# Batched matrix product on one core: an uneven store moves from batch 11 to batches 1 and 2

## The chip, the cores and the metric

The kernel runs on one core of a Trainium2 chip. The metric is the device time of one execution in microseconds; the time before is 124.91 us, the median of three runs (124.76 to 125.31). A profile of one execution and its trace stand beside the times. Engines are named as the profile names them: PE (TensorE), DVE (VectorE), ACT (ScalarE), POOL (GpSimd), SP (SyncE). The 16 DMA engines that move data between HBM and SBUF are another thing; they are numbered 0 to 15 here.

## The reference

Sixteen independent products of 512 x 512 float32 matrices, the second one transposed:

```python
def setup_inputs():
    batch, m, k, n = 16, 512, 512, 512
    return {
        "a": np.random.randn(batch, m, k).astype(np.float32),
        "b": np.random.randn(batch, n, k).astype(np.float32),
    }

def reference(a: np.ndarray, b: np.ndarray) -> np.ndarray:
    return np.matmul(a, b.transpose(0, 2, 1)).astype(np.float32)
```

33.6 MB are read and 16.8 MB are written.

## The kernel before

The sixteen batches go in eight pairs (the variable `u`). A load brings both matrices of a pair from one input, 2 MB in rows of 16 KB per partition: load `2u` is the pair's part of `a`, load `2u + 1` its part of `b` (line 86). Seven load slots of `ld` hold them (`NL`), each with its own semaphore. DVE casts a load to bf16 in three pieces (lines 154 to 158), PE transposes 128 x 128 blocks into `tp` (line 223), ACT copies the transposed `a` into `ta` (line 181), DVE the transposed `b` into `tb` (line 168). Then PE multiplies, 32 matmuls for a pair (line 242), and ACT evicts each bank of `ps` into the output buffer `ob` (line 201). `ob` has seven slots (`NO`); batch `n` uses slot `n % 7`, so that the eviction of batch `n` waits until the store of batch `n - 7` has landed (line 198).

The order of work is written out by hand. Each engine has its own list of instructions:

- ACT issues load 0 and loads 2 to 6 at the start, and later loads `2u + 7` and `2u + 8` after its copies of pair `u`'s transposes (lines 192 to 194), ahead of the evictions of that pair. SP issues load 1.
- POOL waits for each load and passes this on to DVE by the semaphore `s_go` (line 108), one load after the other.
- SP waits until load 7 has landed (line 120) and then stores the batches in order, each when ACT has counted it in `s_out` (line 122). A store is one transfer of 1 MB: partition `p` holds output rows `4p` to `4p + 3`, 8 KB that lie together in HBM. The last row of batch 15 is stored apart, at the end (line 263).

Batch 11 (`X`) is stored in parts. Rows 1 and 2 of all partitions are one SP transfer. Rows 0 and 3 of each partition (2 KB each) are divided by partitions: 32 to 95 in one SP transfer; 0 to 15 in four SP transfers of four partitions each, 16 to 19 in a fifth; 20 to 31 and 96 to 127 in eight transfers that POOL issues, in groups of three and eight partitions (lines 112 to 118). Ahead of each pair of these POOL reads five partitions of 128 bytes into `turn`, which nothing uses; this moves on the DMA engine at which POOL's next transfer begins. SP's parts count in `s_x`, POOL's in `s_y`; ACT waits for both at the end of the program (lines 257 and 258), together with the stores of the last seven batches.

`landed(n)` gives the semaphore and the count that show batch `n` stored. `store` makes a transfer from `ob`.

Of the kernel before, what the change touches and what calls it, by code (L numbers as in the profile page):

```python
# [10 lines left out]
def kernel(  # L11
# [6 lines left out]
    nc = tc.nc  # L18
    P = 128
    batch, M, K = a.shape  # L20
    _, N, _ = b.shape
    J = M // P
# [3 lines left out]
    pairs = batch // 2  # L26
    f32 = mybir.dt.float32
    bf16 = mybir.dt.bfloat16
    NL = 7
    NO = 7  # L30
    X = 11

    def sbuf(name, shape, dtype):
        return ctx.enter_context(nc.sbuf_tensor(name, shape, dtype))

    def sem(name):
        return tc.alloc_semaphore(name)

    with tc.tile_critical(no_gpsimd_drain=True):  # L41
# [8 lines left out]
        ob = sbuf("ob", [P, NO, J, N], f32)  # L50
        turn = sbuf("turn", [P, 4, 2, 16], f32)
# [4 lines left out]
        s_ld = [sem(f"s_ld{i}") for i in range(NL)]  # L56
        s_st = [sem(f"s_st{i}") for i in range(NO)]

        s_go = sem("s_go")
# [11 lines left out]
        s_out = sem("s_out")  # L71
        s_x = sem("s_x")
        s_y = sem("s_y")
# [5 lines left out]
            out=ident[:], in_=ident[:], compare_op=mybir.AluOpType.not_equal, fill=1.0,  # L79
# [6 lines left out]
        def load(n, engine):  # L86
            u, slot = n // 2, n % NL
            src = (a if n % 2 == 0 else b)[2 * u:2 * u + 2].rearrange(
                "e (p j) k -> (e p) j k", j=2 * J
            )  # L90
            engine.dma_start(ld[:, slot], src).then_inc(s_ld[slot], 16)

        def landed(n):
            return s_st[n % NO], 16 * (n // NO + 1)

        def store(n, lo=0, hi=J, step=1, part=slice(0, P), engine=nc.sync):
            rows = slice(lo, hi, step)
            return engine.dma_start(  # L98
                out[n].rearrange("(p j) n -> p j n", j=J)[part, rows], ob[part, n % NO, rows]
            )  # L100

        load(0, nc.scalar)
# [1 line left out]
        for n in range(2, NL):  # L104
            load(n, nc.scalar)

        for n in range(2 * pairs):
            nc.gpsimd.wait_ge(s_ld[n % NL], 16 * (n // NL + 1)).then_inc(s_go, 1)  # L108

        nc.gpsimd.wait_ge(s_out, X + 1)
        for i in range(4):
            nc.gpsimd.dma_start(  # L114
                turn[:5, i], a[0, :5, :64].rearrange("p (x k) -> p x k", x=2)[:, :, :16]
            ).then_inc(s_y, 16)
            for part in (slice(20 + i, 32, 4), slice(96 + i, P, 4)):
                store(X, step=J - 1, part=part, engine=nc.gpsimd).then_inc(s_y, 16)

        nc.sync.wait_ge(s_ld[0], 32)  # L120
        for n in range(batch):
            nc.sync.wait_ge(s_out, n + 1)
            if n != X:
                store(n, hi=J if n < batch - 1 else J - 1).then_inc(landed(n)[0], 16)
                continue


            store(n, lo=1, hi=J - 1).then_inc(landed(n)[0], 16)
            store(n, step=J - 1, part=slice(32, 96)).then_inc(s_x, 16)
            for i in range(4):  # L130
                store(n, step=J - 1, part=slice(i, 16, 4)).then_inc(s_x, 16)
            store(n, step=J - 1, part=slice(16, 20)).then_inc(s_x, 16)

        def taker(engine):
            return lambda s, n: engine.wait_ge(s, n).then_inc(s, -n)  # L135
# [9 lines left out]
        with nc.Fori(0, pairs, engines=[dve]) as u:  # L145
            for x, (h, w, s_c, s_w) in enumerate(
# [4 lines left out]
                if x == 0:  # L151
# [4 lines left out]
                    out=h[:, J:, :], in_=src[:, J:, :HK]  # L156
                ).then_inc(s_c, 1)
                nc.vector.tensor_copy(out=w[:], in_=src[:, :, HK:]).then_inc(s_w, 1)  # L158
            for ko in range(KO):
# [5 lines left out]
                if ko == 1:  # L165
# [3 lines left out]
                    out=tb[:, ko, :],  # L169
# [7 lines left out]
        for u in range(pairs):  # L177
            for ko in range(KO):
                nc.scalar.wait_ge(s_ta, KO * u + ko + 1)
                for e in range(2):  # L180
                    c = nc.scalar.copy(  # L181
                        out=ta[:, ko, e * J * P:(e + 1) * J * P].rearrange(
                            "k (j p h) -> k j p h", j=J, h=2
                        ),
                        in_=tp[:, ko % 2, :, e * HP:(e + 1) * HP].rearrange(
                            "k (h j) p -> k j p h", h=2
                        ),
                    )
                c.then_inc(s_ea, 1)


            for n in (2 * u + NL, 2 * u + NL + 1):
                if n < 2 * pairs:
                    load(n, nc.scalar)
            for e in range(2):
                n = 2 * u + e
                if n >= NO:
                    nc.scalar.wait_ge(*landed(n - NO))
                for j in range(J):
                    nc.scalar.wait_ge(s_mm, J * n + j + 1)  # L200
                    c = nc.scalar.copy(  # L201
                        out=ob[:, n % NO, j, :].rearrange("m (p j) -> m p j", j=2 * J),
                        in_=ps[:, j, :].rearrange("m (j p) -> m p j", j=2 * J),
                    )
                    if e == 0:
                        c.then_inc(s_pv, 1)
                    elif j in (0, J - 1):
                        c.then_inc(s_out, 1)
# [4 lines left out]
        with nc.Fori(0, pairs, engines=[pe]):  # L213
            with nc.Fori(0, 2, engines=[pe]):

                for x, (h, s_c, s_t, s_e) in enumerate(
# [3 lines left out]
                    for g in range(2):  # L220
                        take(s_e, 1)
                        for j in range(2 * J):
                            t = nc.tensor.transpose(  # L223
                                tp[:, 2 * x + g, j, :], h[:, j, g * P:(g + 1) * P], ident[:]
                            )
# [6 lines left out]
            for e in range(2):  # L232
                for jj in range(0, J, 2):
                    if e == 1:
                        take(s_pv, 2)
                    for kk in range(0, KO, 2):
                        for j in (jj, jj + 1):
                            for ko in (kk, kk + 1):
                                if (e, jj, j) == (0, 0, 0) and ko >= 2:
                                    nc.tensor.wait_ge(s_ea, ko - 1)  # L240
                                    nc.tensor.wait_ge(s_eb, ko - 1)
                                t = nc.tensor.matmul(  # L242
                                    ps[:, j, :],
                                    ta[:, ko, (e * J + j) * P:(e * J + j + 1) * P],
                                    tb[:, ko, :].rearrange("k (j p) -> k j p", j=2 * J)[
                                        :, :, e * HP:(e + 1) * HP
                                    ],
                                    start=(ko == 0),
                                    stop=(ko == KO - 1),
                                )  # L250
# [3 lines left out]


    with tc.tile_critical(sync_engine=act, no_gpsimd_drain=True):
        nc.scalar.wait_ge(s_x, 16 * 6)
        nc.scalar.wait_ge(s_y, 16 * 12)
        for n in range(batch - NO, batch):
            nc.scalar.wait_ge(*landed(n))  # L260
    waits = nc.cur_bb.bb.instructions[-1]
# [38 lines left out]
```

## Time and profile before

| | us |
|---|---|
| time, median of 3 runs | 124.91 |
| the profiled execution's own time | 125.12 |
| its span, first to last instruction | 123.3 |
| PE busy | 90.2 (73%) |
| DVE busy | 67.9 (55%) |
| ACT busy | 67.9 (55%) |
| POOL busy | 8.5 (7%) |
| load to landing, median | 29.1 (`a`), 26.8 (`b`) |
| 1 MB store to landing, median | 29.0 |
| last load issued, last load landed | 66.68, 99.78 |
| store of batch 14, of 15, of its last row issued | 111.38, 113.54, 114.33 |
| last landing | 122.19 |

The span is cut into 40 slices of 3.08 us; a digit is a busy share in tenths, and the DMA row is the mean of the 16 DMA engines. The profile counts three DMA queues: loads on ACT's queue (q10: 31.46 MB), stores and load 1 on SP's (q1: 18.70 MB), POOL's transfers on a software queue (q0: 0.18 MB). In the waits, "waited for: us in total, times, longest us" stand behind the arrow. A bracket at the end of a timeline line is the time that the engine stood idle before, and what released it; DVEq is DVE's own sequencer, which waits for semaphores. Besides these views the trace keeps a record of each DMA packet.

### The profile page before, as it was taken

How to read it: one execution, taken by the hardware profiler on the slowest of the kernel's cores; microseconds unless marked ns; L12 is line 12 of the kernel's file. 1: busy time of each engine (PE TensorE's matmuls, PEld its weight loads, DVE VectorE, ACT ScalarE, POOL GpSimd, SP SyncE). 2: the span in 40 equal slices, each digit the busy share in tenths (PEclk: the TensorE clock that was granted, in tenths of full speed). 3: DMA queues.
4: the chain of work that ended last, by engine and by line, in shares of the span. 5: the costliest groups of instructions: out<-in, count | busy, mean ns of one | idle time of the engine just before them, and what ended most of it. 6: DMA issues, size and time to landing. Idle time of an engine off the chain costs nothing. (4 is left out here: it accounts for less than half of the span.)

```text
span 123.3 us, 2255 instructions
## 1 busy us (share of the span) xinstructions
PE 90.2 (73%) x768; PEld 54.8 (44%) x768; DVE 67.9 (55%) x96; ACT 67.9 (55%) x130; POOL 8.5 (7%) x18
## 2 busy tenths in 40 slices
PE   0000089999999899989998999999799917996000
PEld 0000078447744764574477347645654506542000
DVE  0000598982896589388918974872977059400000
ACT  0400064567855966696589468765866069656000
POOL 2000000000000000000000000000000039910000
PEclk9999999999999999999999999999999999999965
DMA  4999999999999999999999999999999999999991
GB/s 112 404 425 425 441 431 431 431 431 441 425 436 425 425 361 415 444 423 425 431 433 425 431 423 425 436 444 428 423 423 441 412 423 423 432 397 432 425 407 72
DMA packets 5341, 50.35 MB, mean 408 GB/s; under 512 B 904, under 2 KB 904, under 8 KB 1500
## 3 DMA queue, kind: packets, MB, share of 16 engines
q10 hardware_dynamic: 2160, 31.46, 60.5%
q1 hardware_dynamic: 2796, 18.70, 36.2%
q0 software_dynamic: 384, 0.18, 0.5%
q14 instruction: 1, 0.01, 0.0%
HBM read 33.56 MB, written 16.78 MB: 408 GB/s over the span
## 5 line engine op out<-in xcount | busy, mean ns | idle before, releaser
L242 PE MATMUL ps<-tb,ta 128*128 128x512 bf16 x256 | 57.8, 379 | 0.4
L201 ACT COPY ob<-ps 128x512 f32<-128x512 f32 x64 | 34.2, 591 | 27.8 <-PE ps L242 21.9
L181 ACT COPY ta<-tp 128x512 bf16<-128x512 bf16 x64 | 33.0, 612 | 13.7 <-PE tp L223 13.2
L242 PEld LDWEIGHTS ps<-tb,ta 128*128 128x128 bf16 x256 | 24.1, 98 | 30.6 <-issue 4.0
L223 PE MATMUL tp<-ident,ha 128*128 128x128 bf16 x256 | 18.6, 224 | 18.7 <-PEq L135 18.2
L223 PEld LDWEIGHTS tp<-ident,ha 128*128 128x128 bf16 x256 | 15.8, 100 | 22.3 <-issue 20.5
L168 DVE COPY tb<-tp 128x1024 bf16<-128x1024 bf16 x32 | 21.2, 685 | 3.6 <-DVEq L135 3.6
L223 PE MATMUL tp<-ident,hb 128*128 128x128 bf16 x256 | 17.6, 223 | 3.5 <-PEq L135 3.3
L223 PEld LDWEIGHTS tp<-ident,hb 128*128 128x128 bf16 x256 | 15.4, 100 | 4.7 <-issue 4.4
L154 DVE CAST ha<-ld 128x1024 bf16 x8 | 5.5, 690 | 14.6 <-POOLq L108 13.8
L163 DVE COPY ha<-wa 128x2048 bf16<-128x2048 bf16 x8 | 5.5, 691 | 12.7 <-DVEq L135 12.7
L154 DVE CAST hb<-ld 128x1024 bf16 x8 | 5.5, 689 | 7.9 <-DVEq L135 7.9
L158 DVE CAST wa<-ld 128x2048 bf16 x8 | 9.8, 1220 | 0.0
L158 DVE CAST wb<-ld 128x2048 bf16 x8 | 9.8, 1220 | 0.0
L114 POOL DMA_DIRECT2D turn<-in_a_dram x4 | 2.7, 663 | 98.9 <-ACT ob L201 98.9
L155 DVE CAST ha<-ld 128x1024 bf16 x8 | 5.5, 687 | 0.0
L155 DVE CAST hb<-ld 128x1024 bf16 x8 | 5.5, 686 | 0.0
L167 DVE COPY hb<-wb 128x2048 bf16<-128x2048 bf16 x8 | 5.5, 684 | 0.0
L98 POOL DMA_DIRECT2D out_dram<-ob x8 | 5.2, 651 | 0.0
L176 ACT ACT_TABLE_LOAD x1 | 1.3, 1283 | 4.1 <-issue 4.1
L78 POOL TENSOR_SCALAR_AFFINE_SELECT ident<-ident 128x128 bf16<-128x128 bf16 x1 | 0.3, 288 | 0.2 <-POOL ident L76 0.2
L76 POOL MEMSET ident<- 128x128 bf16 x1 | 0.2, 205 | 0.5 <-SPq L41 0.5
(5 smaller groups left out, 0.6 us busy)
## 6 DMA issues: line engine op xcount, KB each, us to landing
ld<-in_a_dram ACTq DMA_DIRECT2D x8, 2048.0 KB, 29.1
ld<-in_b_dram ACTq DMA_DIRECT2D x7, 2048.0 KB, 26.8
out_dram<-ob SPq DMA_DIRECT2D x14, 1024.0 KB, 29.0
ld<-in_b_dram SPq DMA_DIRECT2D x1, 2048.0 KB, 12.5
out_dram<-ob SPq DMA_DIRECT2D x1, 768.0 KB, 8.0
out_dram<-ob SPq DMA_DIRECT2D x1, 512.0 KB, 24.5
out_dram<-ob SPq DMA_DIRECT2D x2, 256.0 KB, 7.9
out_dram<-ob POOLq DMA_DIRECT2D x4, 32.0 KB, 6.0
```

Source lines behind the costliest of these rows:

```text
L98: return engine.dma_start(out[n].rearrange("(p j) n -> p j n", j=J)[part, rows], ob[part, n % NO, rows])
L114: nc.gpsimd.dma_start(turn[:5, i], a[0, :5, :64].rearrange("p (x k) -> p x k", x=2)[:, :, :16]).then_inc(s_y, 16)
L154: nc.vector.tensor_copy(out=h[:, :J, :], in_=src[:, :J, :HK])
L155: nc.vector.tensor_copy(out=h[:, J:, :], in_=src[:, J:, :HK]).then_inc(s_c, 1)
L158: nc.vector.tensor_copy(out=w[:], in_=src[:, :, HK:]).then_inc(s_w, 1)
L163: nc.vector.tensor_copy(out=ha[:], in_=wa[:]).then_inc(s_ca, 1)
L167: nc.vector.tensor_copy(out=hb[:], in_=wb[:]).then_inc(s_cb, 1)
L168: nc.vector.tensor_copy(out=tb[:, ko, :], in_=tp[:, 2 + ko % 2].rearrange("k j p -> k (j p)"),).then_inc(s_eb, 1)
L181: c = nc.scalar.copy(out=ta[:, ko, e * J * P:(e + 1) * J * P].rearrange("k (j p h) -> k j p h", j=J, h=2), in_=tp[:, ko % 2, :, e * HP:(e ...
L201: c = nc.scalar.copy(out=ob[:, n % NO, j, :].rearrange("m (p j) -> m p j", j=2 * J), in_=ps[:, j, :].rearrange("m (j p) -> m p j", j=2 * J),)
L223: t = nc.tensor.transpose(tp[:, 2 * x + g, j, :], h[:, j, g * P:(g + 1) * P], ident[:])
L242: t = nc.tensor.matmul(ps[:, j, :], ta[:, ko, (e * J + j) * P:(e * J + j + 1) * P], tb[:, ko, :].rearrange("k (j p) -> k j p", j=2 * J)[:, ...
```

## The change

`X` becomes 1. Batch 11 is stored like any other batch, in one transfer. Batches 1 and 2, which lie in neighbouring slots of `ob`, are stored together by `store_two`, in transfers whose rows are the 8 KB of one partition and one batch. The partitions are divided as follows: SP stores 32 to 95 in one transfer, and 0, 4, 8, 12 and 1, 5, 9, 13 in two more, when batch 2 is counted. POOL stores the rest in ten transfers, with three small reads into `turn` between them (`spare`): six of these thirteen after it has passed on load 7 and batch 2 is counted, seven after it has passed on load 8. In POOL's list this stands between the passing on of loads; before, it stood behind them all.

ACT waits for all these parts (`s_x` 48, `s_y` 208) before it evicts batch 8 into the slot of batch 1; batch 9 has no wait of its own. The two waits at the end of the program are gone. `landed` counts one store less for slots 1 and 2.

```diff
-    X = 11
+    X = 1
...
         def landed(n):
-            return s_st[n % NO], 16 * (n // NO + 1)
-
-        def store(n, lo=0, hi=J, step=1, part=slice(0, P), engine=nc.sync):
-            rows = slice(lo, hi, step)
+            return s_st[n % NO], 16 * (n // NO + (n % NO not in (X, X + 1)))
+
+        def store(n, lo=0, hi=J):
+            return nc.sync.dma_start(
+                out[n].rearrange("(p j) n -> p j n", j=J)[:, lo:hi], ob[:, n % NO, lo:hi]
+            )
+
+        def store_two(part, engine):
+
             return engine.dma_start(
-                out[n].rearrange("(p j) n -> p j n", j=J)[part, rows], ob[part, n % NO, rows]
+                out[X:X + 2].rearrange("e (p j) n -> p e (j n)", j=J)[part],
+                ob[part, X % NO:X % NO + 2].rearrange("p e j n -> p e (j n)"),
             )
...
+        spares = 0
+
+        def spare(*parts):
+            nonlocal spares
+            for part in parts:
+                if isinstance(part, int):
+                    t = nc.gpsimd.dma_start(
+                        turn[:part, spares % 3],
+                        a[0, :part, :64].rearrange("p (x k) -> p x k", x=2)[:, :, :16],
+                    )
+                    spares += 1
+                else:
+                    t = store_two(slice(*part), nc.gpsimd)
+                t.then_inc(s_y, 16)
+
         for n in range(2 * pairs):
             nc.gpsimd.wait_ge(s_ld[n % NL], 16 * (n // NL + 1)).then_inc(s_go, 1)
-
-
-
-        nc.gpsimd.wait_ge(s_out, X + 1)
-        for i in range(4):
-            nc.gpsimd.dma_start(
-                turn[:5, i], a[0, :5, :64].rearrange("p (x k) -> p x k", x=2)[:, :, :16]
-            ).then_inc(s_y, 16)
-            for part in (slice(20 + i, 32, 4), slice(96 + i, P, 4)):
-                store(X, step=J - 1, part=part, engine=nc.gpsimd).then_inc(s_y, 16)
+            if n == X + 6:
+                nc.gpsimd.wait_ge(s_out, X + 2)
+                spare(5, (20, 32, 4), (96, P, 4), 5, (21, 32, 4), (97, P, 4))
+            elif n == X + 7:
+                spare((2, 32, 4), (98, P, 4), (3, 32, 4), (99, P, 4), 8, (16, 17), (17, 18))
 
         nc.sync.wait_ge(s_ld[0], 32)
         for n in range(batch):
             nc.sync.wait_ge(s_out, n + 1)
-            if n != X:
+            if n == X + 1:
+                for part in (slice(32, 96), *(slice(i, 16, 4) for i in range(2))):
+                    store_two(part, nc.sync).then_inc(s_x, 16)
+            elif n != X:
                 store(n, hi=J if n < batch - 1 else J - 1).then_inc(landed(n)[0], 16)
-                continue
-
-
-            store(n, lo=1, hi=J - 1).then_inc(landed(n)[0], 16)
-            store(n, step=J - 1, part=slice(32, 96)).then_inc(s_x, 16)
-            for i in range(4):
-                store(n, step=J - 1, part=slice(i, 16, 4)).then_inc(s_x, 16)
-            store(n, step=J - 1, part=slice(16, 20)).then_inc(s_x, 16)
...
                 n = 2 * u + e
-                if n >= NO:
+                if n == X + NO:
+                    nc.scalar.wait_ge(s_x, 16 * 3)
+                    nc.scalar.wait_ge(s_y, 16 * 13)
+                elif n >= NO and n != X + 1 + NO:
                     nc.scalar.wait_ge(*landed(n - NO))
...
     with tc.tile_critical(sync_engine=act, no_gpsimd_drain=True):
-        nc.scalar.wait_ge(s_x, 16 * 6)
-        nc.scalar.wait_ge(s_y, 16 * 12)
         for n in range(batch - NO, batch):
             nc.scalar.wait_ge(*landed(n))
```

## The prediction

> **What bounds the kernel now.** I read the page's slices first, then the windows of the last 25 us, then the waits, and last the trace's records of single DMA packets.
>
> ```profile
> DMA  4999999999999999999999999999999999999991
> GB/s 112 404 425 425 441 431 431 431 431 441 425 436 425 425 361 415 444 423 425 431 433 425 431 423 425 436 444 428 423 423 441 412 423 423 432 397 432 425 407 72
> ```
>
> The 16 DMA engines are busy from the first slice to the last; no slice between is below 9 tenths. The end of such a kernel is the moment at which the engine with most work finishes. The windows of the tail say so more closely (window, then length, busy time of PE, PEld, DVE, ACT and POOL, clock, DMA share, GB/s):
>
> ```profile
> 99.00:107.00 8.00, 4.58 (x56) 3.28 (x55) 6.12 (x9) 6.07 (x12) 6.44 (x10) 1.00 1.01 426
> 107.00:115.00 8.00, 5.83 (x27) 2.44 (x25) 0.00 (x0) 4.30 (x8) 1.39 (x3) 1.00 1.03 420
> 115.00:121.00 6.00, 0.00 (x0) 0.00 (x0) 0.00 (x0) 0.00 (x0) 0.00 (x0) 0.76 0.95 395
> 121.00:123.30 2.30, 0.00 (x0) 0.00 (x0) 0.00 (x0) 0.00 (x0) 0.00 (x0) 0.50 0.02 9
> ```
>
> From 115 us nothing computes and the DMA share is still 0.95; after 121 it is 0.02, which is one engine working alone. So compute leads the end by some us, and loads and stores that queue behind each other set it. The waits show where compute leans on DMA:
>
> ```profile
> ACT ob L201 <- DMA out_dram<-ob: 5.9, 2, 4.4
> ```
> ```profile
> 99.84 2.05 ACT L201 COPY ob<-ps 128x512 f32<-128x512 f32 x4 [4.42 <-DMA out_dram<-ob]
> ```
> ```profile
> 100.13 0.69 DVE L154 CAST hb<-ld 128x1024 bf16 x1 [4.79 <-DVEq L135]
> ```
>
> ACT waits for batch 6's store (landed 99.82), and the last pair's second cast for load 15 (landed 99.78). From that cast to the last eviction (ends 113.51) is a fixed chain of 13.4 us.
>
> **Engine by engine.** The trace has start, length, queue and bytes of each packet, but not its engine. On a busy engine a packet starts 4 ns before the one ahead ends, and every engine carries the same order of packets on each queue; with these two rules the packets fall into 16 chains without a gap. Batch 11's edge rows label them: four chains (engines 0 to 3) have ten 2 KB packets more; one has neither these nor 4 KB packets of GpSimd's queue (engine 4); eleven have the latter. Their last packets end, in us:
>
> ```
> engine 4              121.73
> engines 0 to 3        120.80  120.84  121.05  121.16
> the other eleven      120.45 to 120.77, and one 121.10
> ```
>
> Engine 4 is last by 0.57 us over the next and by about 1 us over most, though batch 11 already spares it 16 KB. Its packets are longer: its 16 KB packets took 1.95 us above 611 ns each in sum (others mostly 1.1 to 1.4, one 1.57), its 8 KB packets 1.01 us above 309 (others under 0.12).
>
> **What the Trainium skill says.** "DMA: Bandwidth & Descriptors", section "Why a DMA increments its semaphore by 16 and not by 1": the slowest dimension above 1 sets k, the number of engines; SP's transfers use the lowest k engines, GpSimd's take k in a row from a cursor. The chains of before agree: SP's four-partition transfers fell on four chains, GpSimd's groups of 5, 3 and 8 on the rest as described. Section "Queues, rings and completion order": an engine serves its queues in turn. The trace agrees: between 55 and 99 us a 16 KB load (611) and an 8 KB store (309) alternate, and 8 x (611 + 309 - 8) ns = 7.3 us is the spacing of the landings. Section "Latency and other measured facts": GpSimd's first byte comes after about 1 us; here it took 4.6 us (issue 100.56, first packet 105.20), and the measurement decides.
>
> **The change, part by part.** Packets: 8 KB 309 ns, 4 KB 159, 2 KB 84 (medians of the packet records). The path is each engine's sum.
> 1. Batch 11 in one transfer: 8 x 309 = 2472 ns per engine. Now engines 0 to 3 carry 8 x 159 + 18 x 84 = 2784, engine 4 8 x 159 + 8 x 84 = 1944, the others 12 x 159 + 8 x 84 = 2580.
> 2. Batches 1 and 2 together are now 16 x 309 = 4944 ns on every engine. After: SP's 64-partition part gives each engine 8 packets, its two four-partition parts 4 more to engines 0 to 3; GpSimd's parts (5 / 3 / 8 twice, then four times 8) 4 to engines 0 to 3, 4 to engine 4, 8 to 5 to 15. The two one-partition parts have 2 as slowest dimension, so one 8 KB packet each on engines 8, 9 and 10, 11. That is 16 packets on most, 12 on engine 4, 17 on 8 to 11.
> 3. Sums: engine 4 (2472 - 1944) - 4 x 309 = -0.71 us; engines 0 to 3 -0.31; 5 to 7 and 12 to 15 -0.11; 8 to 11 -0.11 + 0.31 = +0.20. New ends: engine 4 121.02; engines 0 to 3 at most 120.84; the others 120.3 to 120.97; the one at 121.10 is among 8 to 15 (its first GpSimd packet comes with theirs), so 121.00 or, as one of 8 to 11, 121.31. Last end: 121.02 or 121.31, against 121.73: -0.71 or -0.42.
> 4. SP's wait order: batch 1's store waits for batch 2. Both are done before SP is released (load 7 lands at 42.7, SP's first store is at 42.72), so nothing. Stores 3 to 15 move past one DMA more (three parts for two stores; a four-partition part took SP 0.62 to 0.74 us where its queue was not full); store 0 is being served then for 7 us, so nothing. At batch 11 six DMAs become one, in a stretch (87 to 95 us) in which SP's next store is due only at 100.45: nothing. The two waits that leave the end were met by 114.6 us, long before the last landing: nothing.
> 5. GpSimd: 10 DMAs with data and 3 small reads (8 and 4 at the tail before, 0.56 to 1.14 us each): 6 after load 7 (42.8 to 47.6 or so), 7 after load 8 (48.6, perhaps 1 us later, to 53 to 57). Queued behind them are the go signals of loads 8 and 9, needed by DVE at 57.03 and 59.37: hidden, with 2 us to spare. Uncovered, it would delay one pair in a stretch that is load-bound from 85 us on.
> 6. The new wait of batch 8's eviction for all parts. Queued behind it on ACT: its evictions, load 15's issue not (ahead of it). Engines 0 to 3 have 20 store packets from SP instead of 16: landed(1) now 61.4 to 62.5, plus 4 x 0.92 us, plus 4 GpSimd packets of 0.31: 66 to 67.5. GpSimd's last part: issue up to 57, 4.6 us, some turns: 63 to 65. ACT gets there at 69.19: hidden by 2 us.
> 7. What moves. GpSimd's 8 or 9 packets take turns from the loads, 8 x 0.305 = 2.4 us (8 to 11: 2.7; engine 4: 1.2). Load 15 lands at 102.2 to 102.5 instead of 99.78, and the whole chain of the last pair is 2.4 to 2.7 later: store 14 is issued at 113.8 to 114.1 (now 111.38), the last eviction ends near 116. Stores get what loads lose: batch 6's landing comes at about 96, and ACT's 4.4 us go, but load 15 takes their place. This costs nothing as long as engines still have stores ahead of 14. They begin store 14 at 115.50 to 116.20 now (engine 4 116.78); with the sums above from about 115.4. Issue to first packet is 1.0 to 1.4 us on idle engines (load 0: 0.92 to 1.96 and 2.35) and 3.6 us at least for store 0, amid loads (42.72 to 46.35). I take 1.4, since store 14 queues behind store 13 on its own ring: 115.2 to 115.5, just in time. With 3.6 it is rival 2.
>
> Engine 4's long packets last until 114.3, when compute and GpSimd's queue end; 2.4 us more of this, at some 25 ns per packet, is up to 0.2 us back. So -0.71 to -0.35; I take **-0.55 us**: span 123.3 to 122.75, the profiled execution's 125.12 to 124.57, and, taking the median to differ from it by the same 0.21 us, 124.91 to **124.36**.
>
> **Rivals.** (1) The weight isn't on engine 4 in ordinary runs, or 8 to 11 become last. For it: a lag of 0.57 us is within what start-up gives one chain (the one at 121.10 lost 0.97 us on its first packet). Against it: engine 4's lag grows steadily, 0.99 to 1.83 us against the median from store 0 to store 6. Gain 0.1 less 0.2: 124.8 to 125.1. (2) **The tail runs dry: slower.** Place: between store 13 and store 14. It decides once load delay plus issue latency exceed 4.6 us (111.38 + 4.6 = 116.0: dry at 115.5 plus 0.45 us that most chains have in hand over the last). With 2.5 + 3.6 store 14 starts at 117.5, most engines stand 1.9 us and end at 122.5 instead of 121.73: 125.7. Against it: store 0's 3.6 us were spent behind load packets. (3) It doesn't do what it says: GpSimd's cursor stands elsewhere, engine 4 gets full work: 121.73 + 0.53 = 122.26, so 125.44.
>
> **How the numbers follow.** About 0.5% (0.62 us) is what a measurement of this kernel can tell from no change. Forecast 0.58 (of it 0.30 beyond 0.62 us, 0.28 within), rival 1 0.16 (no change), rival 2 0.20 (0.17 slower, 0.03 within), rival 3 0.06 (half and half). Faster 0.30, same 0.50, slower 0.20. The range runs from the forecast's best (0.86 us less, with a last end at 120.87, where the other chains' ends lie: 124.05) to rival 3's 125.45 and leaves out rival 2.
>
> **What would show it.** Right: no lone engine after 121 us; GpSimd's queue active around 47 to 62 us with 8 KB packets; load 15 landing near 102.3; ACT no longer waiting for a store; store 14 issued near 113.9; DMA share still 9 in slice 38. Wrong: a dip in the DMA row near 116 us (rival 2), ACT waiting at batch 8, or the last landing as late as now (rival 1).

## The result and the profile after

The changed kernel takes 129.63 us (median of six runs, 128.44 to 129.89), the kernel before 124.92: a ratio of 1.035 (95% interval 1.0315 to 1.0392). The forecast was 124.36, with 125.45 as its upper end. The profiled execution after is the quickest of its runs, 128.44 us with a span of 126.6.

The page after, slices of 3.17 us, first the granted PE clock, then the DMA share and rate:

```profile
PEclk9999999999999999999999995589999999999996
DMA  4999999999999999999999999999999999995293
GB/s 135 404 435 419 424 440 440 430 419 424 440 430 430 430 334 448 432 417 409 417 427 437 425 433 419 432 437 427 443 404 453 401 430 427 422 430 241 124 415 124
```

The DMA row now has a hole near the end (5, 2, with 241 and 124 GB/s). The windows of the tail, with the columns explained above, place it:

```profile
107.00:115.00 8.00, 7.55 (x82) 5.10 (x80) 3.90 (x7) 6.15 (x13) 0.00 (x0) 1.00 1.01 424
115.00:121.00 6.00, 5.04 (x24) 2.07 (x22) 0.00 (x0) 3.81 (x8) 0.00 (x0) 1.00 0.40 168
121.00:126.60 5.60, 0.00 (x0) 0.00 (x0) 0.00 (x0) 0.00 (x0) 0.00 (x0) 0.80 0.63 253
```

Before, compute was over at 115 us and DMA ran full up to 121; now DMA stands at 0.40 in that window while PE and ACT still work. Compute has become what the end waits for. The last eviction ends at 120.7 instead of 113.5 us. The waits and ACT's timeline say where those 7.2 us came from:

```profile
ACT ob L219 <- DMA out_dram<-ob: 10.5, 1, 10.5
```
```profile
67.88 1.09 ACT L196 COPY ta<-tp 128x512 bf16<-128x512 bf16 x2
79.51 2.05 ACT L219 COPY ob<-ps 128x512 f32<-128x512 f32 x4 [10.54 <-DMA out_dram<-ob]
...
91.59 1.07 ACT L219 COPY ob<-ps 128x512 f32<-128x512 f32 x2 [1.16 <-PE ps L260]
```

One wait of 10.54 us, at the first eviction of batch 8: the wait that the change adds. From there the batches with even numbers follow each other every 11.5 us (91.59, 103.05, 114.52), which is compute's own pace (batches 8 and 10 of the kernel before began at 69.19 and 80.66), up to the end. Of the 10.5 us, 3.3 are taken from waits that compute had later before (5.9 us for stores, and those for the last loads); 7.2 remain at the last eviction. The last landing moves less, from 122.19 to 125.59 us, because fewer stores are still queued behind that eviction (8.7 us from it to the last landing before, 4.9 now).

What it waited for is POOL's transfers. In POOL's timeline and in the list of issues (KB each, us from issue to landing):

```profile
53.02 1.59 POOL L103 DMA_DIRECT2D out_dram<-ob  x2
```
```profile
out_dram<-ob POOLq DMA_DIRECT2D x6, 128.0 KB, 17.8
turn<-in_a_dram POOLq DMA_DIRECT2D x2, 0.6 KB, 9.8
out_dram<-ob POOLq DMA_DIRECT2D x2, 16.0 KB, 25.4
turn<-in_a_dram POOLq DMA_DIRECT2D x1, 1.0 KB, 23.6
```

The last issue ends at 54.6 us, so issuing was as quick as forecast. A read of 1 KB needed 23.6 us, longer than a store of 128 KB; but eight stores stand ahead of it in POOL's queue, so this alone doesn't tell whether their bytes or their packets are the delay. The last of POOL's thirteen transfers lands at 79.45, 0.06 us before ACT goes on. The queue line counts the packets, then the MB; first the kernel before, then the changed one:

```profile
q0 software_dynamic: 384, 0.18, 0.5%
```
```profile
q0 software_dynamic: 544, 0.92, 1.9%
```

544 packets are 34 on each of 16 engines. Only 112 carry 8 KB and 18 carry 128 bytes; all others have 4 or 8 bytes. POOL's packets run from 48.5 to 79.1 us: 30.6 / 34 = 0.90 us each, and one load packet plus one store packet is 0.611 + 0.309 - 0.008 = 0.91. Threaded into chains as in the prediction, the packets of this trace show it one by one: in 524 of the 528 stretches between two POOL packets of one engine stand exactly one load packet and one store packet.

**The theory:** an engine serves its three queues in turn, packet by packet, and every packet of POOL's queue, a 4-byte one too, waits for one load packet and one store packet. Each POOL transfer gives every engine two packets, or three where it moves pairs of 8 KB rows, whether or not the engine carries any of its data. Eight such stores, three reads and two transfers of one partition make 8 x 3 + 3 x 2 + 2 x 2 = 34.

**Rivals:** POOL's queue is slow by bytes, or by transfer wherever it stands; or the later loads and a tail that runs dry after them are the loss.

### The profile page after: what moved, and what is told of

It is laid out like the page before. It is cut to its first block, busy times and chain, and to the rows that moved or that the text cites. A ratio compares the mean times of both kernels' runs of the same rounds, so it can differ in the third digit from the quotient of the medians.

```text
span 126.6 us, 2250 instructions
## 1 busy us (share of the span) xinstructions
PE 92.3 (73%) x768; PEld 56.1 (44%) x768; DVE 67.9 (54%) x96; ACT 67.9 (54%) x130; POOL 9.4 (7%) x19
## 5 line engine op out<-in xcount | busy, mean ns | idle before, releaser
L260 PE MATMUL ps<-tb,ta 128*128 128x512 bf16 x256 | 59.3, 385 | 9.0 <-PEq L150 8.5
L241 PE MATMUL tp<-ident,ha 128*128 128x128 bf16 x256 | 19.6, 230 | 18.3 <-PEq L150 17.7
L241 PEld LDWEIGHTS tp<-ident,ha 128*128 128x128 bf16 x256 | 16.6, 103 | 22.0 <-issue 20.3
L241 PEld LDWEIGHTS tp<-ident,hb 128*128 128x128 bf16 x256 | 15.9, 102 | 1.0 <-issue 0.7
L103 POOL DMA_DIRECT2D out_dram<-ob x10 | 6.8, 686 | 2.3 <-DMA ld<-in_a_dram 2.3
L123 POOL DMA_DIRECT2D turn<-in_a_dram x3 | 1.9, 628 | 42.0 <-DMA ld<-in_b_dram 42.0
```

Of the source, the lines that this page charges most:

```text
L103: return engine.dma_start(out[X:X + 2].rearrange("e (p j) n -> p e (j n)", j=J)[part], ob[part, X % NO:X % NO + 2].rearrange("p e j n -> p ...
L123: t = nc.gpsimd.dma_start(turn[:part, spares % 3], a[0, :part, :64].rearrange("p (x k) -> p x k", x=2)[:, :, :16],)
L241: t = nc.tensor.transpose(tp[:, 2 * x + g, j, :], h[:, j, g * P:(g + 1) * P], ident[:])
L260: t = nc.tensor.matmul(ps[:, j, :], ta[:, ko, (e * J + j) * P:(e * J + j + 1) * P], tb[:, ko, :].rearrange("k (j p) -> k j p", j=2 * J)[:, ...
```

## Experiments

**e1_free: the wait taken away.** Batches 8 and 9 are evicted into load slot 2, which no load fills after load 9, and stored from there.

```diff
+        def place(n):
+            if n in (X + NO, X + 1 + NO):
+                x = J * (n - X - NO)
+                return ld[:, 2, x:x + J]
+            return ob[:, n % NO]
...
-                if n == X + NO:
+                if n == X + 2 * NO:
                     nc.scalar.wait_ge(s_x, 16 * 3)
```

> The changed kernel, but batches 8 and 9 are evicted into load slot 2 (free since load 9 was cast), so that batch 8 no longer waits for the parts of batches 1 and 2; batch 15 waits for them instead. Theory (that wait is the whole loss): ACT stands nowhere near 69 us, POOL's queue still ends near 79, load 15 lands near 102.5, the last eviction ends near 116, 124.2 to 124.8 us. Rival (the loads that are 2.5 us later, and a tail that runs dry after them, are the loss): stays above 127 us, with a dip in the DMA row before the end.

Measured: 124.91 us against 125.08 of the kernel before beside it, ratio 0.9984 (0.9974 to 0.9993). POOL's queue is as late as ever (last landing 79.25), but ACT goes on at once, and the hole at the end is gone:

```profile
68.84 1.07 ACT L225 COPY ld<-ps 128x512 f32<-128x512 f32 x2 [1.11 <-PE ps L266]
```
```profile
DMA  4999999999999999999999999999999999999992
```

All 4.7 us of the loss are that wait; without it the change is 0.2 us faster than the kernel before (0.1 us short of the range expected). The rival of the dry tail falls: load 15 lands at 102.37 and store 14 is issued at 113.99, as the prediction had it, and no engine stands.

**e2_more: packets without bytes.** Four more reads of 640 bytes at the end of POOL's transfers, waited for like the rest.

```diff
-                spare(... 8, (16, 17), (17, 18))
+                spare(... 8, (16, 17), (17, 18), 5, 5, 5, 5)
```

> The changed kernel with four more 5-partition reads of 128 bytes at the end of POOL's transfers, 2.5 KB in all. Theory (each POOL transfer costs every engine two or more turns, whatever it carries, 0.91 us each while loads and stores are queued): 8 more turns, POOL's last landing 7.3 us later, near 86.7, batch 8's wait near 18 us, 136 to 137.5 us. Rival (POOL's queue is short of bandwidth, bytes count): no change, 129.6 us.

Measured: 136.04 us, ratio 1.087 (1.083 to 1.092). POOL's queue and ACT's wait:

```profile
q0 software_dynamic: 672, 0.92, 1.9%
```
```profile
ACT ob L219 <- DMA turn<-in_a_dram: 18.0, 1, 18.0
```

672 / 16 = 42 packets, 8 more, and the wait grows from 10.5 to 18.0 us: 0.9 us for each, with the megabytes unchanged. The last landing is at 86.27.

**e3_late: the same transfers at the tail.** `X` becomes 11, POOL's thirteen transfers stand behind all loads, and the program's end waits for them.

```diff
-    X = 1
+    X = 11
...
-            if n == X + 6:
-                nc.gpsimd.wait_ge(s_out, X + 2)
-                spare(...)
-            elif n == X + 7:
-                spare(...)
+        nc.gpsimd.wait_ge(s_out, X + 2)
+        spare(...)
+        spare(...)
```

> The same thirteen POOL and three SP transfers, but for batches 11 and 12 at the tail, where no load is queued and nothing waits for them but the end. Theory (a POOL packet waits for one packet of each other queue): 34 packets at 0.31 us instead of 0.91, about 10 to 13 us from first to last, ended by 118; 124.2 to 124.7 us. Rival (POOL's queue takes 2.3 us per transfer wherever it stands): 30 us from 105, so 136 us and more.

Measured: 125.47 us, ratio 1.0027 (1.0017 to 1.0036). The same 544 packets now take from 105.7 to 117.3 us, 0.34 us each. The loads are over by then (load 15 lands at 100.14), so that only store packets are left to stand before them. The last landing is 117.6. POOL's queue is not slow by transfer. The time is 0.8 us above what was expected. In the profiled execution six 8 KB packets stretch near 116 us, two of them POOL's, which took 0.89 and 1.10 us instead of 0.31; whether they, or the engines that carry most (see e6_fixed), are the 0.8 us stays open.

**e4_plain: no unevenness at all.** The kernel before with batch 11 as one transfer.

```diff
-            if n != X:
-                store(n, hi=J if n < batch - 1 else J - 1).then_inc(landed(n)[0], 16)
-                continue
...
+            store(n, hi=J if n < batch - 1 else J - 1).then_inc(landed(n)[0], 16)
```

> The kernel before with batch 11 in one transfer and no POOL transfer: every engine has the same bytes. Theory of the prediction (engine 4 is slower and last): its end moves from 121.73 to 122.26, 125.4 us. Rival (engine 4's lag is no more than one execution's start-up, and in ordinary runs it isn't last): 124.6 to 125.0 us.

Measured: 125.15 us, ratio 1.0011 (0.9998 to 1.0025). That lies between the two expectations. All the sparing of engine 4 in the kernel before is worth 0.1 us over these runs (by the interval at most 0.3), not 0.5. One chain has long packets in this trace too (0.77 us at 55 to 100 and 0.66 after, against at most 0.05 in the others), so the slow engine is real; but it ends at 121.70, not 122.26. Part of the difference is start-up: load 6 has left this chain at 41.54 us here and at 41.83 in the profile of before, and the other chains with it. The rest is not: at the end it lags the median chain by 1.22 us here and by 1.07 there, where the bytes (0.53 us more on it, 0.11 less on most others) ask for 0.64 of difference. With one execution of each, the cause of that stays open.

**e5_few: the change's place and bytes with few packets, the wait kept.** All engines even.

```diff
-                for part in (slice(32, 96), *(slice(i, 16, 4) for i in range(2))):
+                for part in (slice(32, 96), slice(0, 16)):
...
-                spare(5, (20, 32, 4), (96, P, 4), 5, (21, 32, 4), (97, P, 4))
+                spare((16, 32), (96, P))
```

> The changed kernel, batch 8's wait and all, but every engine gets the same: SP stores partitions 32 to 95 and 0 to 15, POOL 16 to 31 and 96 to 127, of both batches, in two transfers each; POOL still moves 768 KB. Theory (packets of POOL's queue count, not bytes): 3 + 5 packets per engine instead of 34, 7 us, last landing near 57; batch 8 waits for nothing; loads late by some 2 us as in the changed kernel; 125.0 to 125.4 us, as with even stores. Rival (POOL's queue is limited by bytes): last landing near 74, batch 8 waits 5 us, 126 us and more.

Measured: 125.47 us, ratio 1.0036 (1.0023 to 1.005). POOL's queue:

```profile
q0 software_dynamic: 128, 0.79, 1.6%
```

Nearly as many megabytes as after the change (0.79 against 0.92) in 8 packets per engine: they have landed at 57.66, and no wait for a store is left in ACT's list. The theory's number holds (57 was expected). The time is 0.1 us beyond what was expected.

**e6_fixed: the two one-partition transfers.** Threading e1_free's packets into engines as for the prediction (engines 0 to 3 are the four chains with SP's four-partition parts, engine 4 the one with the fewest bytes) shows two chains **of engines 0 to 3** with six 8 KB packets from POOL and two with four, engine 4 with four, and the other eleven with eight each, where four of them should have nine. The two end last, at 121.30 and 121.45; engine 4 ends at 120.57. So the 32 KB went to two of engines 0 to 3, not to 8 to 11. This kernel is e1_free with those two partitions in eight SP transfers of four 1 KB rows.

```diff
+                for p in (16, 17):
+                    for m in (X, X + 1):
+                        for lo in (0, N // 2):
+                            store_quarters(p, m, lo).then_inc(s_x, 16)
```

> The kernel of e1_free, but partitions 16 and 17, which POOL stored in two transfers of one partition each, go by SP in eight transfers of four rows of 1 KB, a row to each of engines 0 to 3. Theory (those two transfers put all four 8 KB rows on two of engines 0 to 3, not on 8 to 11, and these two finish last): the last engine ends 0.3 to 0.4 us earlier than in e1_free, 124.5 to 124.7 us. Rival (start-up differences decide which engine is last): no change against e1_free, 124.9 us.

Measured: 125.26 us, ratio 1.0006 (0.9988 to 1.0024), and a wide spread (124.57 to 126.08, and one run of 127.20). Neither side of the expectation can be read off it, because the edit brought a wait of its own, by the very mechanism under test: engines 0 to 3 get 16 more packets (eight rows, eight semaphore writes) on SP's queue, each behind a load packet. In the profiled execution (125.96 us) store 3 lands at 84.5 instead of 75.0, and batches 10 and 11 wait for their slots:

```profile
84.57 2.06 ACT L235 COPY ob<-ps 128x512 f32<-128x512 f32 x4 [4.55 <-DMA out_dram<-ob]
91.87 2.05 ACT L235 COPY ob<-ps 128x512 f32<-128x512 f32 x4 [5.25 <-DMA out_dram<-ob]
```

**e7_two and e8_four: engine 4 spared by few transfers, the wait kept.** In e7_two SP stores 112 partitions, then four, then one; POOL makes one read to move on and one transfer of eleven partitions, one to each of engines 5 to 15.

```diff
-                spare(5, (20, 32, 4), (96, P, 4), 5, (21, 32, 4), (97, P, 4))
+                spare(5, (116, 127))
...
-                for part in (slice(32, 96), *(slice(i, 16, 4) for i in range(2))):
+                for part in (slice(0, 112), slice(112, 116), slice(127, P)):
```

e8_four does this twice on POOL's side (32 KB off engine 4) and has eight of e6_fixed's small SP transfers for the two partitions left over.

> The changed kernel with few POOL transfers and its wait kept: SP stores 0 to 111, 112 to 115 and 127, POOL reads five partitions and stores 116 to 126 in one transfer, 16 KB off engine 4. Theory: 5 POOL packets per engine, last landing near 54, no wait at batch 8; the last engine near 121.2; 124.6 to 124.9 us. Rival (any splitting of batches 1 and 2 costs more than it brings): above 125.1 us.

> As e7_two with 32 KB off engine 4: SP stores 32 to 127, 22 to 25, 26 to 29, and 30 and 31 in eight transfers of four 1 KB rows; POOL reads five partitions and stores 0 to 10, and again with 11 to 21. Theory: 10 POOL packets per engine, last landing near 60, no wait at batch 8; the last engine near 121.0; 124.4 to 124.7 us, the best of all. Rival (with 16 KB off, engine 4 is no longer last, so the second 16 KB bring nothing): equal to e7_two.

Measured: e7_two 124.81 us, ratio 0.9977 (0.9967 to 0.9987), faster than both given kernels. Its median is the lowest of all kernels here, but e1_free's 0.9984 (0.9974 to 0.9993) can't be told from it, and what of its 0.3 us is owed to engine 4 was not tested. e8_four 129.44 us, ratio 1.036 (1.033 to 1.039), a miss by 5 us. The same line of ACT in both, e7_two first:

```profile
70.30 2.29 ACT L217 COPY ob<-ps 128x512 f32<-128x512 f32 x4 [1.62 <-DMA out_dram<-ob]
```
```profile
78.76 2.05 ACT L227 COPY ob<-ps 128x512 f32<-128x512 f32 x4 [10.66 <-DMA out_dram<-ob]
```

Neither should have waited. POOL's transfers of e7_two have landed at 54.03 and those of e8_four at 59.96, as expected; it is SP's small ones that land at 78.74, against 70.28 for SP's parts in e7_two. Some sixteen packets more on engines 0 to 3, 8.5 us: 0.53 us each, about a load packet. The theory was applied to POOL's queue and forgotten for SP's, where it holds as well. Whether the second 16 KB off engine 4 bring anything stays open.

**e9_reads: the delay without the change.** The kernel before, all its stores untouched, with twenty more POOL reads of 640 bytes, for which batch 8 waits.

```diff
             nc.gpsimd.wait_ge(s_ld[n % NL], 16 * (n // NL + 1)).then_inc(s_go, 1)
+            if n in (7, 8):
+                for i in range(10):
+                    nc.gpsimd.dma_start(turn[:5, 10 * (n - 7) + i], ...).then_inc(s_z, 16)
...
+                if n == NO + 1:
+                    nc.scalar.wait_ge(s_z, 16 * 20)
```

> The kernel before, stores and all, with twenty more reads of five partitions, 128 bytes each, by POOL (ten after load 7, ten after load 8), and batch 8's eviction waits for them too. They move 12.5 KB. Theory (two packets per engine and transfer, each waiting for one load and one store packet): 40 packets at 0.91 us, last landing near 84 to 85, batch 8 waits some 15.5 us, loads no later than before; 133.5 to 135 us. Rival (the split of the stores, the bytes of POOL's queue or the later loads are what costs): landed by 60, 125.1 us.

Measured: 131.77 us (two runs), ratio 1.053 (1.050 to 1.057).

```profile
q0 software_dynamic: 1024, 0.20, 0.8%
```
```profile
ACT ob L210 <- DMA turn<-in_a_dram: 13.6, 1, 13.6
```

640 packets more, 40 per engine, for 12.5 KB, and a wait of 13.6 us. The loads are not late (load 15 lands at 100.37). This is the loss of the change without any part of it but its small packets and its wait. It ended 1.7 us below the range expected: a packet took 0.85 us, not 0.91, and the end moved less than the wait.

**e10_late_two, e11_seven, e12_whole: the place.** e10_late_two makes e7_two's five transfers for batches 11 and 12 at the tail. As it came out slower, e11_seven keeps only a division like its own (SP alone: 112 partitions, seven to an engine, then 16, one to an engine), and e12_whole only the joining of two batches (SP alone: 128).

```diff
-                for part in (slice(0, 112), slice(112, 116), slice(127, P)):
+                for part in (slice(0, 112), slice(112, P)):
```

> The five transfers of e7_two for batches 11 and 12 instead of 1 and 2, so that no wait inside the program and no load is touched. Theory (in e7_two nothing of the gain comes from the place, all from 8 KB rows and 16 KB off engine 4): as e7_two, 124.7 to 125.0 us. Rival (the early place helps by itself, since stores get ahead of the loads): above e7_two, 125.1 us or more.

> Batches 11 and 12 together by SP alone: partitions 0 to 111 in one transfer[...] and 112 to 127 in another (one to an engine); no POOL transfer, all engines even. Theory (in e10_late_two the division into sevens stretches the packets[...]): packets of 8 KB well above 309 ns in the mean at 108 to 116 us, as in e10_late_two (380 to 392), 126.5 to 128 us. Rival (POOL's transfer and the uneven load did it): 125.0 to 125.4 us.

> The control to e11_seven: batches 11 and 12 together by SP in one transfer of all 128 partitions. Theory: 309 ns per packet, as even as single stores, 125.0 to 125.4 us. Rival (storing two batches together at the tail is what costs): as e11_seven, 126.5 us and more.

Measured: 127.47 us, ratio 1.019 (1.016 to 1.023); 127.20, 1.021 (1.016 to 1.026); 125.16, 1.0011 (0.9997 to 1.0024). Windows of e10_late_two at the tail:

```profile
107.00:111.00 4.00, 3.95 (x19) 1.79 (x19) 0.00 (x0) 2.15 (x4) 0.00 (x0) 1.00 1.03 360
111.00:115.00 4.00, 2.12 (x10) 0.78 (x8) 0.00 (x0) 2.15 (x4) 0.00 (x0) 1.00 1.00 326
```

The engines are fully busy at 326 to 360 GB/s instead of some 425: 8 KB packets of SP's queue take 380 to 392 ns in the mean at 108 to 116 us (309 otherwise), single ones up to 1.6 us. e11_seven has the same (385 ns at 112 to 116 us), e12_whole does not. So it is the division and not the joining of batches, and POOL isn't needed for it.

The expectation of e11_seven blamed the sevens, and its number came true by another way. Threaded into chains, the 224 packets of its 112-partition transfer take 314 ns in the mean, as good as undisturbed. The 32 packets of the second transfer, partitions 112 to 127, take 646 ns in the mean and up to 2.1 us; they make 10.8 of the 12.9 us by which the 8 KB packets from there on run over. In e10_late_two the first to stretch are those of POOL's eleven neighbouring partitions (from 106.9 us, up to 1.07 us), and only then SP's. What both runs share is neighbouring partitions stored one to an engine. POOL's parts whose partitions lie four apart stretch far less: of their transfers' 112 packets none takes over 0.33 us in the changed kernel, and three take over 0.4 in e3_late, where stores run alone. A kernel with the sixteen partitions alone was not run.

## Why the prediction was wrong

- **The step that failed is 6**, the new wait at batch 8. It gave POOL's last part "issue up to 57, 4.6 us, some turns: 63 to 65". Issue and latency held (54.6; first packets at 48.5); "some turns" should have been 34 packets at 0.91 us. The count could have been read before: the profile of before had 384 packets in POOL's queue line, 24 per engine, for twelve transfers of which at most four gave an engine data. Step 7 counted only the 8 or 9 packets with data. e2_more, e3_late, e5_few and e9_reads change the number of packets, their place and the bytes one by one, and the delay follows the packets and what stands between them.
- The cover of "2 us" was thus one of -10.5, and nothing was said of the price if it failed. It was 4.7 us, the difference between the changed kernel and e1_free.
- **Step 7 held in what it says of the loads and the tail.** The loads came 2.6 to 2.9 us later (said: 2.4 to 2.7): load 15 landed at 102.71 after the change and at 102.37 in e1_free (said: 102.2 to 102.5). Store 14 at 113.99 (said: 113.8 to 114.1), "just in time", and no engine ran dry. Rival 2 had the right sign by luck and the wrong place: the hole in the DMA row came from ACT's late start on batch 8.
- **Step 2 was wrong on the one-partition transfers.** They were placed by the rule for the number of engines; the traces of three kernels (after, e1_free, e2_more) have them on two of engines 0 to 3. The Trainium skill, "DMA: Bandwidth & Descriptors", section "Why a DMA increments its semaphore by 16 and not by 1", names an exception: some direct copies that POOL issues run on all sixteen engines, with the partitions per engine rounded up, so that the last engines can be left without data. Two rows that fall each time on the same two low engines fit that, but no run here tells which two, nor why these transfers and not the others.
- **The size of the gain was too large.** Without the wait, 0.2 us instead of 0.55. Engine 4 did become one of the early ones (120.57, said 121.02), but two of engines 0 to 3 took its place at the end, and in e4_plain rival 3's price of 0.53 us for not sparing it measured 0.1 over fourteen runs. Rival 1 was nearer than the forecast here.
- Step 3 carries the error of step 2: the last engine of e1_free ends at 121.45 (said: 121.02 or 121.31). Steps 1, 4 and 5 are not contradicted: SP and POOL issued in time, the go signals were no hindrance.

## What to carry to other kernels

Count packets, not bytes, for every queue that shares the DMA engines with a bulk stream: in these runs a small transfer paid one bulk packet of each other queue per packet, its semaphore writes included, on every engine that it touched (POOL's touched all sixteen). Where something waits for such transfers, make them few, put them where the other queues are short, or give the waiting work another buffer. A plan that deals bytes to chosen engines needs a trace of where they went, and the last engine of one execution need not be what sets the time of many.

## What had not been expected of the hardware

After its 8.5 us without work at 72 to 81 us PE came back at a lower clock (the 5, 5, 8 of the PEclk row). Sixteen matmuls of the same shape before and after the gap:

```profile
68.37 3.83 PE L260 MATMUL ps<-tb,ta 128*128 128x512 bf16 x16
...
80.73 4.91 PE L260 MATMUL ps<-tb,ta 128*128 128x512 bf16 x16 [8.53 <-PEq L150]
```

The profiled execution had a mean clock of 0.964, the six others 0.942 to 0.955 and 129.2 to 129.9 us; that the clock is what sets them apart was not tested.

Where stores run alone, a transfer of sixteen neighbouring partitions, one to each engine, stretched its 8 KB packets from 309 to 646 ns in the mean (e11_seven). Amid loads it happened less evenly: of the packets of POOL's eleven neighbouring partitions 15 of 44 took over 0.4 us in e8_four (up to 1.65), and 2 of 22 in e7_two. The Trainium skill, "SBUF — State Buffer", section "Door 1: The DMA port swizzle", says that partitions reach SBUF's DMA ports in groups of four neighbours, so that partitions 112 to 127 put sixteen engines on four ports. The traces agree with that, without showing a port.
